# Output projection of a hybrid decoder layer: 14 of 16 column tiles by seven half-size products per pair of tiles instead of eight

## The chip, the core and the metric

One core of one Trainium2 chip runs one launch. The metric is device microseconds of that launch; here the median of three runs, with one further execution recorded by the hardware profiler. Engines by the names of the profile: PE (TensorE, with PEld for its weight loads), DVE (VectorE), ACT (ScalarE), POOL (GpSimd), SP (the queue that issues most DMAs).

## What is computed

One layer of a decoder trunk on 512 prompt tokens and 8 sample tokens (520 columns), width 2048. One input projection feeds two branches, a gated mixing of chunks (`y_a`) and a matrix-state recurrence (`y_b`); then

```python
merged = sigmoid(g_a) * (y_a @ p_a) + sigmoid(g_b) * (y_b @ p_b)
out = x + c_gate[:, None] * (merged @ w_out)
y = rmsnorm(out, final_g)
```

The change is in how `merged @ w_out` is computed, a product of 2048 x 2048 weights with 2048 x 520 values. `c_gate` is one column for the prompt and one for each of the 8 sample tokens.

## The kernel before

Values are kept transposed: 128 features by 520 tokens per tile, 16 tiles per 2048 features. Each big product is a `job`: one column tile of 128 outputs, cut into units of four k-tiles. For a unit a weight load of 128 x 8 x 128 (two units in one) comes by SP's queue into `raw`; `split_to` makes a high part by a cast on ACT (`hi`) and the rest by a subtract on DVE (`lo`, or POOL where said), both of 128x512. Per k-tile and half of the tokens (260 columns) PE does three matmuls: hi by high values, hi by low values, lo by high values. So a job with 16 k-tiles is 96 matmuls. Two PSUM banks take the two halves; an `evac` function is called for each.

The order of all instructions is written out by the program: `emit_pe` (line 401) walks the units; before the matmuls of unit i it issues the weight loads up to unit i+8, as long as one of four `raw` buffers is free, and the splits up to unit i+2 (four `hi` and four `lo` buffers). Work beside the matmuls is written as generators; `side.tick()` after each k-tile lets those go on whose time, by a table of costs in the program (`Engine.cost`, line 140), has come, and `side.drain` (line 95) runs one to its end on the spot. Every engine works its own queue in that order, and an instruction that waits holds up all behind it.

The last stages: the tail of the input projection (17 jobs of gates, beside the last pair of the recurrence and the sample task), then 16 jobs `pa` of 8 k-tiles, 16 jobs `pb` of 16, then 16 jobs `wo`. `pre_merge` (1404) drains all tasks ahead of `pa`. `evac_pb` (1443) adds the two gated branches of tile m and splits the 520 columns into `mh` and `ml`, the values for `wo`. `evac_out` (1482) does out = x + gate * product on DVE (prompt columns by one `scalar_tensor_tensor`, the 8 sample columns by two small operations), and `square` (1496) squares on ACT, scales by `final_g` and adds the square to `acc` on DVE. The first 13 `wo` jobs do both halves; the last three (`n_last`) do all first halves and then all second halves, so that the norm and the output of the first half (`final_norm(0)`, 1507, and `rows`, 1531) run beside the last three second halves. All instructions go through one helper, so that the trace gives L136 for nearly all of them; tiles tell them apart.

Of the kernel before, what the change touches and what calls it, by code (L numbers as in the profile page):

```python
# [173 lines left out]
def hybrid_step(ctx, tc, xT, cT, wc, vecs, sst, win, wlr, w2a2, stw, lnv, wsT, w00, bs, pa, pb, wo,  # L174
# [64 lines left out]
    def C(shape, name, dt=F32):  # L239
        return const.tile(list(shape), dt, name=name)  # L240
# [4 lines left out]
    hs = slots("h", 32)  # L245
    gelp = open_pool("g", "gel")
# [37 lines left out]
    def rounded(t, name):  # L284
        r = C((128, 128), name, F32R)
        V.tensor_copy(r, t)
        return r

    bones_r, vmat_r, cmat_r = rounded(bones, "bonesr"), rounded(vmat, "vmatr"), rounded(cmat, "cmatr")
    mask = C((128, 128), "mask")  # L290
# [75 lines left out]

    ptr = dict(dma=0, split=0, pe=0)
    raws = [4]

    def emit_dma(upto):  # L370
        while ptr["dma"] < min(len(units), upto):
            u = units[ptr["dma"]]
            if u["load"]:
                if not raws[0]:
                    return
                raws[0] -= 1
                src, users = u["load"]
                t = wp.tile([128, 8, 128], F32, tag="raw", bufs=4, name="raw")
# [8 lines left out]
                users[-1][0]["frees"] = True  # L387
            ptr["dma"] += 1

    def emit_split(upto):  # L390
        while ptr["split"] < min(len(units), upto):
# [4 lines left out]
            lo = wp.tile([128, u["n"], u["j"]["M"]], F32R, tag="lo", bufs=4, name="lo")  # L396
            split_to(u.pop("raw"), hi, lo, G if 22 <= n < 32 else V)
            raws[0] += u.pop("frees", 0)
            u["hl"] = (hi, lo)

    def emit_pe():
        while ptr["pe"] < len(units):
# [947 lines left out]
    tail += [(win[104 + m], gb_d[m]) for m in range(n_g, 16)]  # L1350
    for n, (w, d) in enumerate(tail):
        job(w, 16, 128, mov_h, evac_gate(d, ws), pre={0: pre_tail0, len(tail) - 2: pre_ya}.get(n))
# [7 lines left out]
    def load_ya():  # L1360

        for m in range(8):
            t = ws(name="yar")
# [3 lines left out]
        for m in range(n_early):  # L1367
            hl = ws(dt=F32R, name="yah"), ws(dt=F32R, name="yal")
# [35 lines left out]
    def pre_merge():  # L1404
        for t in list(tasks.values()):
            side.drain(t)
# [233 lines left out]
```

## Time and profile before

| | |
|---|---|
| runs | 2318.20, 2318.81, 2319.34 us (median 2318.81) |
| profiled execution | 2316.69 us, span of the core 2315.0, mean granted clock 0.996 |
| PE / PEld busy | 2268.9 / 2206.0 us (98% / 95%) |
| DVE / ACT / POOL busy | 1389.1 / 946.2 / 689.5 us (60% / 41% / 30%) |
| `pa` begins, last matmul of `wo` ends | about 1832.7, 2293.4 us |

The span is the time from the core's first to its last instruction. Matmuls overlap in the record, so their busy time says little of their rate; the interval between starts does. "Idle before, releaser" names what ended an engine's wait. One full level of the granted clock (1.00) is 2.4 GHz, 0.50 is 1.2 GHz.

### The profile page before, as it was taken

What the parts mean: (1) busy time and instruction counts of PE and PEld (TensorE: products, weight loads), DVE (VectorE), ACT (ScalarE), POOL (GpSimd) and SP (SyncE); (2) the same over time, 40 slices, a digit from 0 to 9 for tenths busy, and PEclk for the clock granted to TensorE, in tenths of its full rate; (3) what the DMA queues carried; (4) which work ended last, traced back from release to release, by engine and by line L of the source; (5) the groups of instructions that cost most, each with busy time, mean ns of one, the idle gap of its engine ahead of it and who ended that gap; (6) DMA issues with size and microseconds to landing.
All of it is one profiled execution on the core that took longest, in us unless ns stands there. A gap on an engine that the chain in (4) does not pass through costs nothing.

```text
span 2315.0 us, 52544 instructions
## 1 busy us (share of the span) xinstructions
PE 2268.9 (98%) x21339; PEld 2206.0 (95%) x21339; DVE 1389.1 (60%) x2627; ACT 946.2 (41%) x2209; POOL 689.5 (30%) x1517
## 2 busy tenths in 40 slices
PE   7999999999999999999999999999999999999996
PEld 6899999999999999999999999999999999999996
DVE  6655453336767767767767677676898433444436
ACT  4323431234445545445545455455334422223333
POOL 2420002000444423443525444155684320000001
PEclk9999999999999999999999999999999999999998
DMA  8854248432332332232323223232454643334225
GB/s 288 300 212 174 97 140 274 155 101 83 93 92 83 101 97 78 86 95 88 95 82 97 76 93 93 82 100 84 140 167 141 233 158 123 116 117 170 92 92 138
DMA packets 165537, 296.64 MB, mean 128 GB/s; under 512 B 69192, under 2 KB 86344, under 8 KB 164656
## 3 DMA queue, kind: packets, MB, share of 16 engines
q1 hardware_dynamic: 149616, 239.13, 33.2%
q0 software_dynamic: 15680, 54.16, 6.2%
q8 instruction: 168, 2.75, 0.5%
q14 instruction: 73, 0.60, 0.1%
HBM read 264.94 MB, written 28.28 MB: 127 GB/s over the span
## 4 chain that ended last, share of the span: by engine, by line
PE 79%; DVE 3%; issue 1%; POOL 0%; ACT 0%; DVEq 0%; POOLq 0%; ACTq 0%
PE acc L136 67%; PE gram L136 2%; PE y L136 2%; PE S L136 1%; PE R L136 1%; PE U L136 1%; PE lora L136 1%; PE m L136 1%; PE tk L136 1%; PE vT L136 1%; DVE st L136 1%; DVE lo L136 1%; PE t L136 0%; PE nrm L136 0%; POOL mtm L136 0%
## 5 line engine op out<-in xcount | busy, mean ns | idle before, releaser
L136 PE MATMUL acc<-hh,hi 128*128 128x260 f32 (+1 forms) x3904 | 1156.1, 296 | 4.8 <-DVE gel L136 2.3
L136 PE MATMUL acc<-hl,hi 128*128 128x260 f32 (+1 forms) x3904 | 1101.8, 282 | 0.3 <-DVE hl L136 0.3
L136 PE MATMUL acc<-hh,lo 128*128 128x260 f32 (+1 forms) x3904 | 1101.4, 282 | 0.4 <-DVE lo L136 0.4
L136 PEld LDWEIGHTS acc<-hh,hi 128*128 128x128 f32 (+1 forms) x3904 | 734.3, 188 | 28.1 <-issue 9.8
L136 PEld LDWEIGHTS acc<-hl,hi 128*128 128x128 f32 (+1 forms) x3904 | 734.8, 188 | 2.0 <-DVE hl L136 0.6
L136 PEld LDWEIGHTS acc<-hh,lo 128*128 128x128 f32 (+1 forms) x3904 | 733.2, 188 | 0.6 <-DVE lo L136 0.6
L136 DVE TENSOR_TENSOR lo<-raw,hi 128x512 fp32r<-128x512 f32 (+2 forms) x682 | 487.1, 724 | 327.5 <-ACT hi L136 323.5
L136 ACT CAST hi<-raw 128x512 fp32r<-128x512 f32 (+2 forms) x692 | 403.1, 597 | 282.2 <-PE acc L136 267.8
L136 POOL TENSOR_TENSOR mtm<-xm,mtm 128x60 f32<-128x60 f32 (+24 forms) x496 | 189.0, 381 | 137.4 <-DMA xm<-xd 103.3
L136 POOL TENSOR_TENSOR mtm<-mtm 128x60 f32<-128x60 f32 (+24 forms) x496 | 186.9, 377 | 38.8
L136 PE MATMUL acc<-mh,hi 128*128 128x260 f32 x512 | 144.6, 283 | 0.0
L136 PE MATMUL acc<-ml,hi 128*128 128x260 f32 x512 | 144.6, 282 | 0.0
L136 PE MATMUL acc<-mh,lo 128*128 128x260 f32 x512 | 144.6, 282 | 0.0
L136 POOL DMA_DIRECT2D out<-xo x4 | 3.1, 774 | 428.9 <-DVE xo L136 421.4
L136 DVE TENSOR_TENSOR gel<-gel,acc 128x260 f32<-128x260 f32 x160 | 65.3, 421 | 78.7 <-PE acc L136 78.2
L136 ACT ACTIVATE q<-acc,vec 128x260 f32<-128x260 f32 (+1 forms) x100 | 47.6, 476 | 120.9 <-PE acc L136 120.3
L136 PEld LDWEIGHTS acc<-mh,hi 128*128 128x128 f32 x512 | 96.5, 188 | 0.0
L136 PEld LDWEIGHTS acc<-ml,hi 128*128 128x128 f32 x512 | 96.4, 188 | 0.0
L136 PEld LDWEIGHTS acc<-mh,lo 128*128 128x128 f32 x512 | 96.3, 188 | 0.0
L136 ACT COPY xu<-U 64x64 f32<-64x64 f32 x256 | 52.9, 207 | 96.3 <-PE U L136 87.4
L136 PE MATMUL acc<-ybh,lo 128*128 128x260 f32 x320 | 90.3, 282 | 0.0
L136 PE MATMUL acc<-ybl,hi 128*128 128x260 f32 x320 | 90.3, 282 | 0.0
(291 smaller groups left out, 3538.1 us busy)
## 6 DMA issues: line engine op xcount, KB each, us to landing
raw<-in_win SPq DMA_DIRECT2D x240, 512.0 KB, 3.7
wcr<-in_wc POOLq DMA_DIRECT2D x57, 512.0 KB, 7.9
raw<-in_wo SPq DMA_DIRECT2D x38, 512.0 KB, 3.6
wcg<-in_wc SPq DMA_DIRECT2D x64, 256.0 KB, 5.6
raw<-in_pb SPq DMA_DIRECT2D x32, 512.0 KB, 3.7
xm<-xd SPq DMA_DIRECT2D x64, 128.0 KB, 2.7
raw<-in_pa SPq DMA_DIRECT2D x16, 512.0 KB, 3.5
x<-in_xT SPq DMA_DIRECT2D x16, 260.0 KB, 5.3
```

What stands on the lines that cost most here:

```text
L136: return f(*a, **k)
```

## The change

With the weights of a pair of column tiles a, b cut into quarters (A11, A12 the two halves of k for a, A21, A22 for b) and the merged values into quarters (b11, b12 the two halves of tokens of the first eight k-tiles, b21, b22 of the other eight), seven products of 8 k-tiles by 260 tokens replace eight:

S1 = A21+A22, S2 = S1-A11, S3 = A11-A21, S4 = A12-S2; T1 = b12-b11, T2 = b22-T1, T3 = b22-b12, T4 = b21-T2; P1 = A11 b11, P2 = A12 b21, P3 = S4 b22, P4 = A22 T4, P5 = S1 T1, P6 = S2 T2, P7 = S3 T3. With U = P1+P6: a's first half is P1+P2, a's second U+P5+P3, b's first U+P7+P4, b's second U+P7+P5.

The order is P1, P2, P6, P5, P7, P4, P3, two units of 12 matmuls each. Weight sums are done on POOL before the split, by halves; the value quarters are summed and split once, in tasks started by `evac_pb`, whose tiles now come in the order 0, 8, 1, 9, ... 25 of the split pieces are stored to DRAM, 17 of them fetched again when the output stage starts and 8 (b12) for the last two tiles, which are done as before by halves (`n_last` 2). Constants of the recurrence go to a pool of their own, which is given up with the recurrence's pool three jobs before the end of the tail; one pool `fin` then serves to the end, and brings four more `raw` buffers. x is loaded in four tiles, in the last `pb` job.

```diff
-    def C(shape, name, dt=F32):
-        return const.tile(list(shape), dt, name=name)
+    def C(shape, name, dt=F32, pool=None):
+        return (pool or const).tile(list(shape), dt, name=name)
     vec = C((128, V_N), "vec")
     SY.dma_start(out=vec, in_=vecs)
     open_pool("h", "h", "right")
     hs = slots("h", 32)
+    rwc = open_pool("rwc", "rwc")
...
+    PIECES = dict(P1=("A11", "b11"), P2=("A12", "b21"), P6=("S2", "T2"), P5=("S1", "T1"), P7=("S3", "T3"),
+                  P4=("A22", "T4"), P3=("S4", "b22"))
+    def seven(jobs, mov):
+        seq = []
+        for srcs, done in jobs:
+            j = dict(src=dict(A11=srcs[0][:, 0:8], A12=srcs[0][:, 8:16], A21=srcs[1][:, 0:8], A22=srcs[1][:, 8:16]),
+                     done=done, w={}, uses=dict(A11=6, A21=6, A22=4, A12=6, S1=4, S2=4), M=128)
+            seq += [(j, p) for p in ("P1", "P2", "P6", "P5", "P7", "P4", "P3")]
+        at = {}
+        for j, p in seq:
+            at[id(j), p] = len(units)
+            for k0 in (0, 4):
+                units.append(dict(j=j, st=p, k0=k0, n=4, first=k0 == 0, last=k0 == 4, load=None, pre=None, part=None,
+                                  mov=mov))
+        for j in {id(j): j for j, _ in seq}.values():
+            p1, p2, p6 = (at[id(j), p] for p in ("P1", "P2", "P6"))
+            for u, n in ((p1, "A11"), (p1 + 1, "A21"), (p2, "A22"), (p2 + 1, "A12")):
+                units[u]["quarter"] = n, j
+            for u, out, x, y, op, half in (
+                    (p6 - 8, "S1", "A21", "A22", OP.add, 0), (p6 - 8, "S2", "S1", "A11", OP.subtract, 0),
+                    (p6 - 7, "S1", "A21", "A22", OP.add, 1), (p6 - 7, "S2", "S1", "A11", OP.subtract, 1),
+                    (p6 - 6, "S3", "A11", "A21", OP.subtract, 0), (p6 - 5, "S3", "A11", "A21", OP.subtract, 1),
+                    (p2 - 1, "S4", "A12", "S2", OP.subtract, 0), (p2 - 1, "S4", "A12", "S2", OP.subtract, 1)):
+                units[u].setdefault("sums", []).append((j, out, x, y, op, half))
+    HOME = dict(S3="A21", S4="A12")
+    sevens = ["m0", "m1", "m2", "y", "ch"]
+    def used(j, n):
+        n = HOME.get(n, n)
+        j["uses"][n] -= 1
+        if not j["uses"][n]:
+            raw_done(j["w"][n])
+    def weight_sum(j, out, x, y, op, half):
+        if out in ("S1", "S2") and out not in j["w"]:
+            j["w"][out] = raw_tile()
+        w = j["w"]
+        k = slice(4 * half, 4 * half + 4)
+        G.tensor_tensor(w[HOME.get(out, out)][:, k, :], w[x][:, k, :], w[y][:, k, :], op)
+        used(j, x)
+        used(j, y)
...
+    raws = {"w": 4}
+    raw_home = {}
+    def raw_tile():
+        key = max(raws, key=raws.get)
+        raws[key] -= 1
+        t = (wp if key == "w" else cur[key]).tile([128, 8, 128], F32, tag="raw", bufs=4, name="raw")
+        raw_home[t.tensor.name] = key
+        return t
...
+            if (u["load"] or "quarter" in u) and sum(raws.values()) < (3 if "quarter" in u else 1):
+                return
+            if "quarter" in u:
+                n, j = u["quarter"]
+                j["w"][n] = raw_tile()
+                SY.dma_start(out=j["w"][n], in_=j["src"][n])
...
+    def seventh(u, hi, lo):
+        j, p = u["j"], u["st"]
+        if u["first"]:
+            sevens.append(sevens.pop(0))
+            j["ps"] = psum(sevens[-1], 1, "acc")
+        o = j["ps"][:, 0:HN]
+        for k in range(4):
+            mh, ml = u["mov"](PIECES[p][1], u["k0"] + k)
+            first, last = u["first"] and k == 0, u["last"] and k == 3
+            PE.matmul(o, hi[:, k, :], mh, start=first, stop=False)
+            PE.matmul(o, hi[:, k, :], ml, start=False, stop=False)
+            PE.matmul(o, lo[:, k, :], mh, start=False, stop=last)
+            side.tick()
+        if u["last"]:
+            j["done"](p, o)
...
+            for a in u.get("sums", ()):
+                weight_sum(*a)
...
+    def pre_last_home():
+        for t in list(tasks.values()):
+            side.drain(t)
+        cur.pop("wkv").release()
+        cur.pop("rwc").release()
+        open_pool("fin", "fin")
+        raws["fin"] = 4
+        V.tensor_scalar(mod[:, 32:48, :], mod[:, 32:48, :], 0.5, None, OP.mult)
...
+            pre={0: pre_tail0, len(tail) - 3: pre_last_home, len(tail) - 2: pre_ya}.get(n))
...
+    piece, resting = {}, {}
+    SPILLED = [("T3", k) for k in range(7)] + [("T4", k) for k in range(7)] + [("b22", k) for k in range(4, 7)]
+    SPILLED += [("b12", k) for k in range(8)]
+    def keep(n, k, src, eng):
+        t = (fs if (n, k) in SPILLED or n in ("b22", "T3", "T4") else ms)((128, 2, HN), F32R, name=n)
+        split_to(src, t[:, 0], t[:, 1], eng)
+        if (n, k) in SPILLED:
+            resting[n, k] = dram.tile([128, 2, HN], F32, name=f"{n}d{k}")
+            side.unawaited(lambda: SY.dma_start(out=resting[n, k], in_=t.bitcast(F32)))
+        else:
+            piece[n, k] = t
+    def back(n, k):
+        piece[n, k] = t = (ms if n == "b12" else fs)((128, 2, HN), F32R, name=n)
+        SY.dma_start(out=t.bitcast(F32), in_=resting[n, k])
+    def quarters(k, x, y):
+        b11, b12, b21, b22 = x[:, 0:HN], x[:, HN:N], y[:, 0:HN], y[:, HN:N]
+        t = fs((128, 2, HN), name="t12")
+        t1, t2 = t[:, 0], t[:, 1]
+        u = fs((128, 2, HN), name="t34")
+        t3, t4 = u[:, 0], u[:, 1]
+        keep("b11", k, b11, V)
+        G.tensor_tensor(t1, b12, b11, OP.subtract)
+        keep("b21", k, b21, V)
+        yield
+        V.tensor_tensor(t2, b22, t1, OP.subtract)
+        yield
+        keep("T2", k, t2, V)
+        keep("T1", k, t1, V)
+        G.tensor_tensor(t3, b22, b12, OP.subtract)
+        G.tensor_tensor(t4, b21, t2, OP.subtract)
+        yield
+        keep("T3", k, t3, G)
+        yield
+        keep("T4", k, t4, G)
+        yield
+        keep("b22", k, b22, G)
+        yield
+        keep("b12", k, b12, G)
+    def mov_piece(n, k):
+        side.draining = True
+        while (n, k) not in piece:
+            side.clock["PE"] += 333.0
+            side.tick()
+        side.draining = False
+        t = piece[n, k]
+        return t[:, 0], t[:, 1]
+    def mov_half(k, hf):
+        return mov_piece(("b11", "b12", "b21", "b22")[k // 8 * 2 + hf], k % 8)
...
+            V.tensor_tensor(g[:, sl], g[:, sl], m1[m][:, sl], OP.add)
             if hf == 1:
-                gate_t.pop(m)
-                V.tensor_tensor(g, g, m1[m], OP.add)
                 m1[m] = None
-                hi, lo = ms(dt=F32R, name="mh"), ms(dt=F32R, name="ml")
-                A.activation(hi, g, AF.Copy, scale=0.5)
-                V.scalar_tensor_tensor(lo, g, 0.5, hi.bitcast(F32), OP.mult, OP.subtract)
-                mg[m] = (hi, lo)
+                if m >= 8:
+                    side.add(quarters(m - 8, gate_t.pop(m - 8), gate_t.pop(m)))
...
+    for n in range(16):
+        m = n // 2 + n % 2 * 8
+        job(pb[m], 16, 128, lambda k: ybT[k], evac_pb(m), pre=pre_pb(n, m))
...
+    units[-3]["pre"] = load_x(0, 1)
+    units[-2]["pre"] = load_x(2, 3)
...
+        G.memset(fin["acc"], 0.0)
+        A.activation(zero8, zero8, AF.Sqrt)
+        tasks["back"] = side.add(reload())
+    def reload():
+        for i, (n, k) in enumerate(SPILLED[:-8]):
+            while (n, k) not in resting:
+                yield "t"
+            back(n, k)
+            if i % 2:
+                yield "t"
...
+    def part_out(m, hf, o, last=True):
+        sl = slice(hf * HN, hf * HN + HN)
+        n = min(HN, T - hf * HN)
+        a = slice(hf * HN, hf * HN + n)
+        x = fin["x"][m // 4][:, m % 4]
+        V.scalar_tensor_tensor(x[:, a], o[:, 0:n], mod[:, 32 + m, 0:1], x[:, a], OP.mult, OP.add)
+        if n < HN:
+            t = cur["fin"].tile([128, NS], F32, tag="gs", bufs=4, name="gs")
+            V.tensor_tensor(t, o[:, n:HN], mod[:, 32 + m, 1:9], OP.mult)
+            G.tensor_tensor(x[:, T:N], x[:, T:N], t, OP.add)
+        if last:
+            close(m, hf)
...
+    def close(m, hf):
+        sl = slice(hf * HN, hf * HN + HN)
+        tasks["sq", m, hf] = side.add(square(m, fin["x"][m // 4][:, m % 4, sl], fin["acc"][:, sl], hf))
...
-            V.tensor_tensor(acc, acc, q, OP.add)
+            (G if m < 14 and m % 2 else V).tensor_tensor(acc, acc, q, OP.add)
+    def done_out(a, b):
+        st = {}
+        def scaled(m, t, u, sample):
+            s8 = None
+            if sample:
+                s8 = cur["fin"].tile([128, NS], F32, tag="gs", bufs=4, name="gs")
+                G.tensor_tensor(s8, u[:, T - HN:HN], mod[:, 32 + m, 1:9], OP.mult)
+            A.activation(t, u, AF.Identity, scale=mod[:, 32 + m, 0:1])
+            return t, s8
+        def add(m, hf, t, s8):
+            x = fin["x"][m // 4][:, m % 4]
+            n = min(HN, T - hf * HN)
+            G.tensor_tensor(x[:, hf * HN:hf * HN + n], x[:, hf * HN:hf * HN + n], t[:, 0:n], OP.add)
+            if hf:
+                G.tensor_tensor(x[:, T:N], x[:, T:N], s8, OP.add)
+            close(m, hf)
+        def later(f):
+            yield
+            f()
+        def e(p, o):
+            if p == "P1":
+                st["u"] = fs((128, HN), name="u")
+                A.copy(st["u"], o)
+                part_out(a, 0, o, False)
+            elif p == "P2":
+                part_out(a, 0, o)
+            elif p == "P6":
+                V.tensor_tensor(st["u"], st["u"], o, OP.add)
+                st["a"] = fs((128, HN), name="gu")
+                side.add(later(lambda: st.update(a=scaled(a, st["a"], st["u"], True))))
+            elif p == "P5":
+                part_out(a, 1, o, False)
+                part_out(b, 1, o, False)
+            elif p == "P7":
+                V.tensor_tensor(st["u"], st["u"], o, OP.add)
+                def f():
+                    st["b"] = scaled(b, st["u"], st["u"], True)
+                    add(b, 1, *st["b"])
+                tasks["add", b] = side.add(later(f))
+            elif p == "P4":
+                part_out(b, 0, o, False)
+                side.drain(tasks["add", b])
+                add(b, 0, *st["b"])
+            else:
+                part_out(a, 1, o, False)
+                add(a, 1, *st["a"])
+        return e
...
-    n_last = 3
-    for m in range(16 - n_last):
-        job(wo[m], 16, 128, lambda k: mg[k], evac_out(m), pre=pre_out(m))
+    def pre_plain():
+        for k in range(8):
+            back("b12", k)
+    n_last = 2
+    n0 = len(units)
+    seven([((wo[m], wo[m + 1]), done_out(m, m + 1)) for m in range(0, 16 - n_last, 2)], mov_piece)
+    units[n0]["pre"] = pre_out
     for hf in range(2):
         for m in range(16 - n_last, 16):
-            job(wo[m], 16, 128, lambda k: mg[k], evac_out(m), hfs=(hf,),
-                pre=pre_last if hf and m == 16 - n_last else pre_out(m))
+            job(wo[m], 16, 128, None, evac_out(m), hfs=(hf,),
+                pre={(0, 14): pre_plain, (1, 14): pre_last}.get((hf, m)))
+            for u in units[-4:]:
+                u["j"]["half"] = mov_half
```

## Rows read from the trace of the kernel before

**Rows 1.** Page, part 1: busy time, share of the span, instructions of each engine.
```profile
PE 2268.9 (98%) x21339; PEld 2206.0 (95%) x21339; DVE 1389.1 (60%) x2627; ACT 946.2 (41%) x2209; POOL 689.5 (30%) x1517
```

**Rows 2.** Chain that ended last, 1700 to 2315: start, us, what.
```profile
1832.70 443.06 PE acc L136 x3692
...
2276.79 16.58 PE acc L136 x138
```

**Rows 3.** Windows: length, busy and instructions of PE, PEld, DVE, ACT, POOL; clock, DMA share, GB/s.
```profile
60.00:70.00 10.00, 8.00 (x61) 7.29 (x61) 9.93 (x28) 5.20 (x14) 5.23 (x9) 1.00 0.89 323
...
1700.00:1800.00 100.00, 96.03 (x877) 93.82 (x876) 87.25 (x121) 37.26 (x82) 56.91 (x61) 1.00 0.48 154
...
2000.00:2100.00 100.00, 100.00 (x837) 100.00 (x836) 41.16 (x71) 25.09 (x44) 0.00 (x0) 1.00 0.35 114
```

**Rows 4.** Groups by shape, DVE, 2130 to 2290: busy us, mean ns | idle before, releaser.
```profile
L136 DVE TENSOR_TENSOR lo<-raw,hi 128x512 fp32r<-128x512 f32 x66 | 45.1, 688 | 36.3 <-ACT hi L136 36.3
...
L136 DVE SCALAR_TENSOR_TENSOR xo<-acc,mod,xo 128x260 f32<-128x260 f32 x15 | 7.3, 489 | 41.3 <-PE acc L136 41.3
```

**Rows 5.** Groups by shape, ACT, 2130 to 2290.
```profile
L136 ACT CAST hi<-raw 128x512 fp32r<-128x512 f32 x66 | 40.0, 614 | 35.3 <-PE acc L136 34.4 <-DVE xo L136 0.8
L136 ACT ACTIVATE xo<-xo,vec 128x260 f32<-128x260 f32 x29 | 14.9, 513 | 0.9
L136 ACT ACTIVATE osq<-xo 128x260 f32<-128x260 f32 x29 | 12.2, 422 | 62.7 <-DVE xo L136 62.7
```

**Rows 6.** Timeline, POOL: start, us, instruction [idle before, releaser].
```profile
1844.71 1.76 POOL L136 TENSOR_TENSOR ybw<-ybr,ybw 128x520 fp32r<-128x520 f32 x1
...
1846.56 1.31 POOL L136 TENSOR_TENSOR ybw<-ybr,ybw 128x520 fp32r<-128x520 f32 x1
1847.82 0.18 POOL L136 COPY ybr<-ybs 128x8 f32<-128x8 f32 x1
...
2296.08 2.39 POOL L136 TENSOR_TENSOR xo<-xo,rs 128x1040 f32<-128x1040 f32 x1
```

**Rows 7.** Timeline, DVE and POOL, around 1635.
```profile
1634.13 2.85 DVE L136 TENSOR_TENSOR lo<-raw,hi 128x512 fp32r<-128x512 f32 x1
...
1634.37 2.05 POOL L136 TENSOR_TENSOR st<-st 128x512 f32<-128x512 f32 x2
```

**Rows 8.** Groups by shape, DVE: 1835 to 1862 (two), then 1900 to 2100 (two).
```profile
L136 DVE TENSOR_TENSOR lo<-raw,hi 128x512 fp32r<-128x512 f32 x11 | 11.0, 1031 | 0.0
L136 DVE SCALAR_TENSOR_TENSOR m<-gld,acc 128x260 f32<-128x260 f32 x10 | 4.2, 423 | 11.9 <-PE acc L136 11.9
...
L136 DVE TENSOR_TENSOR lo<-raw,hi 128x512 fp32r<-128x512 f32 x70 | 45.3, 687 | 31.6 <-ACT hi L136 31.6
...
L136 DVE SCALAR_TENSOR_TENSOR m<-gld,acc 128x260 f32<-128x260 f32 x9 | 3.8, 425 | 15.8 <-PE acc L136 15.8
```

**Rows 9.** Timeline, SP, at the start of the output projection.
```profile
2107.68 1.98 SPq L136 DMA_DIRECT2D xo<-in_xT  x4
```

**Rows 10.** Windows, DMA at the start of the output projection (last two columns).
```profile
2112.00:2114.00 2.00, 2.00 (x19) 2.00 (x18) 1.90 (x3) 1.23 (x4) 0.00 (x0) 1.00 1.00 424
```

**Rows 11.** Timeline, ACT, DVE and PE, around the end of the sample task.
```profile
1796.39 0.39 ACT L136 ACTIVATE gt<-acc 128x260 f32<-128x260 f32 x1 [1.01 <-PE acc L136]
...
1796.42 0.53 DVE L136 TENSOR_SCALAR say<-say,sbmv,srs 128x64 f32<-128x64 f32 x2
...
1798.71 0.27 PE L136 MATMUL ysT<-ident,say 128*128 128x128 f32 x1
```

**Rows 12.** Timeline, DVE and POOL, behind the last matmul.
```profile
2294.07 0.69 DVE L136 TENSOR_TENSOR xo<-xo,rs 128x520 f32<-128x520 f32 x1
...
2298.76 0.80 POOL L136 DMA_DIRECT2D out<-xo  x1 [0.30 <-POOL xo L136]
```

**Rows 13.** Windows, the end (DMA share is the last but one column).
```profile
2302.00:2305.00 3.00, 0.00 (x0) 0.00 (x0) 2.97 (x4) 0.00 (x0) 1.79 (x1) 0.50 1.15 230
...
2308.00:2311.00 3.00, 0.00 (x0) 0.00 (x0) 0.00 (x0) 0.00 (x0) 0.00 (x0) 0.50 1.24 198
```

More of the change, by code (lines that the diff above doesn't have):

```diff
@@ L289, in hybrid_step @@
     bones_r, vmat_r, cmat_r = rounded(bones, "bonesr"), rounded(vmat, "vmatr"), rounded(cmat, "cmatr")
-    mask = C((128, 128), "mask")
+    mask = C((128, 128), "mask", pool=rwc)
     V.memset(mask, 1.0)
@@ L420, in emit_pe @@
             hi, lo = u.pop("hl")
+            if "st" in u:
+                seventh(u, hi, lo)
+                continue
             if u["first"]:
@@ L1350, in hybrid_step, with four @@
     tail += [(win[104 + m], gb_d[m]) for m in range(n_g, 16)]
+    NF_S = 31
+    def pre_last_home():
[6 more added lines that the diff above has]
+        V.tensor_scalar(mod[:, 32:48, :], mod[:, 32:48, :], 0.5, None, OP.mult)
+    fs = slots("fin", NF_S)
+    def four(name, dt=F32):
+        return cur["fin"].tile([128, 4, N], dt, tag="W", bufs=4, name=name)
     for n, (w, d) in enumerate(tail):
-        job(w, 16, 128, mov_h, evac_gate(d, ws), pre={0: pre_tail0, len(tail) - 2: pre_ya}.get(n))
+        job(w, 16, 128, mov_h, evac_gate(d, lambda **k: (fs if "fin" in cur else ws)(**k)),
+            pre={0: pre_tail0, len(tail) - 3: pre_last_home, len(tail) - 2: pre_ya}.get(n))
     yaT, ybT, mg = [None] * 8, [None] * 16, [None] * 16
@@ L1389, in load_yb @@
         ld = [load(0)]
+        w = None
         for p in range(HP):
@@ L1394, in load_yb @@
             yield 1500.0
-            if p < 6:
-                w = wide("ybw", F32R, 2 * N)
-                hi, lo = w[:, 0:N], w[:, N:2 * N]
+            if p < 8:
+                w = w if p % 2 else four("ybw", F32R)
+                hi, lo = w[:, 2 * (p % 2)], w[:, 2 * (p % 2) + 1]
             else:
-                hi, lo = ws(dt=F32R, name="ybh"), ws(dt=F32R, name="ybl")
+                hi, lo = fs(dt=F32R, name="ybh"), fs(dt=F32R, name="ybl")
             A.copy(hi, t)
@@ L1404, in pre_merge @@
     def pre_merge():
-        for t in list(tasks.values()):
-            side.drain(t)
+        side.drain(tasks["ya"])
         cur["h"].release()
@@ new lines, in hybrid_step, with load_x, pre_out @@
+    fin = {"x": [None] * 4}
+    def load_x(*gs_):
+        def f():
+            for g in gs_:
+                fin["x"][g] = four("xo")
+                SY.dma_start(out=fin["x"][g], in_=xT[:, 4 * g:4 * g + 4, :])
+        return f
+    units[-3]["pre"] = load_x(0, 1)
+    units[-2]["pre"] = load_x(2, 3)
+    def pre_out():
+        ybT.clear()
+        fin["acc"] = fs(name="acc")
+        fin["rs"] = fs(name="rs")
+        G.memset(fin["acc"], 0.0)
+        A.activation(zero8, zero8, AF.Sqrt)
+        tasks["back"] = side.add(reload())
@@ L1504, in square @@
         if m < 15:
-            V.tensor_tensor(acc, acc, q, OP.add)
+            (G if m < 14 and m % 2 else V).tensor_tensor(acc, acc, q, OP.add)
[42 more added lines that the diff above has]
+                add(b, 0, *st["b"])
+            else:
+                part_out(a, 1, o, False)
+                add(a, 1, *st["a"])
+        return e
     def final_norm(hf):
         rs = fin["rs"][:, hf * HN:hf * HN + HN]
-        side.drain(tasks["sq", 14, hf])
+        for m in range(15):
+            side.drain(tasks["sq", m, hf])
         yield from grab()
@@ L1555, in hybrid_step @@
     side.drain(side.add(final_norm(1)))
-    cur["out"].release()
+    cur["fin"].release()
     cur["mrg"].release()
```

92 lines of the change are left out of this document (35 added, 57 removed).

## The prediction, made before the changed kernel was run

> **What bounds the kernel now.** I read the busy lines of the page first: TensorE is busy for 98% of the span [rows 1]. The chain of waits shows where that is the bound: from 1832.70 us to the last matmul it is one unbroken run of TensorE, broken only by the reduction of the first half's norm, and behind it stand 21.6 us of normalising and storing that TensorE has no part in [rows 2]. So a matmul taken out of that run is worth its issue interval, as long as whatever feeds TensorE keeps up. The windows give the interval: 837 matmuls in 100.00 us, 0.1195 us each, at granted clock 1.00 [rows 3]. In the same window VectorE is busy for 41 us of 100 and GpSimd for none. The output projection therefore runs with GpSimd empty; the change fills it.
>
> **What goes.** 14 column tiles cost 14 x 96 = 1344 matmuls, 160.6 us, or 22.9 us per pair. Seven products of 24 matmuls are 168 per pair, 20.1 us, and 140.5 us for seven pairs. 20.1 us are saved if nothing else waits. The same number of weight loads goes with them. The count follows from the code, so that the products are really fewer isn't in question.
>
> **What comes, per pair.** Weight splits rise from 8 to 14, each a ScalarE cast of 0.61 us and a VectorE subtract of 0.69 us [rows 4, 5]: 8.6 and 9.7 us of 20.1, and a unit of weights now lasts 12 matmuls, 1.43 us, instead of 2.87. VectorE's evacuations are six at 0.49, two at about 0.43 and three of 8 columns: about 4.3 us. ScalarE has four squares (0.42) and four scalings (0.51) as before, and two scalings and a copy more [rows 5]: 13.7 us in all. Both fit into 20.1.
>
> GpSimd gets eight half sums of 128x512. Two neighbouring starts of its 128x520 subtract lie 1.26 us apart; 128x1040 takes 2.39 [rows 6], so by the slope 128x260 is about 0.70, an estimate from these two. Eight sums 10.1, three adds and two norm sums of 128x260 3.5, seven pieces of 8 columns at 0.18 [rows 6] 1.3: 14.9 us.
>
> **GpSimd and VectorE get in each other's way.** A VectorE subtract that starts at 1634.13 lasts 2.85 us instead of 0.69: it ends just after the two GpSimd products that ran from 1634.37 to 1636.42 [rows 7]. The other way, the GpSimd subtract goes from 1.31 to 1.76 when a VectorE subtract falls in: 0.45 [rows 6]. Operations with one operand in PSUM are spared: 423 ns beside a busy GpSimd, 425 beside an idle one, while the subtracts go from 687 to 1031 [rows 4, 8]. So each of 14 splits and two norm sums adds up to 0.45 us to GpSimd's 14.9: 22.1 us per pair, already over TensorE's 20.1. The Trainium skill (SBUF — State Buffer, Who interferes with whom) calls this an exclusive lock, held for the whole instruction by a VectorE operation with two SBUF inputs. By that sentence each collision would cost GpSimd 0.69 and not 0.45; with the five collisions counted below that makes 1.2 us more per pair and a time of about 2339.
>
> **Where it reaches TensorE.** The order of the queues decides. From the end of the fourth product (P5), in us, one unit being 1.43: VectorE needs 1.3 for P5's two evacuations, GpSimd 0.2 more, so S1 and S2 of the next pair (first halves) run from 1.5 to 4.0. Only behind them stands what P7's evacuation needs: small product 0.18, ScalarE's scaling 0.51, add 0.70, small add 0.18, done at 5.6. The square of that result is queued on ScalarE ahead of the cast for P3's second unit, as ScalarE now sits waiting on squares (62.7 us of idle before 29 of them) [rows 5]. Square, scaling, cast and subtract are 0.42 + 0.51 + 0.61 + 0.69 = 2.23: ready at 7.8, wanted at 7.2. Then S1 and S2 (second halves), the add behind P4, ready at 8.8, and 2.23 later, at 11.0, the second unit of the next P1, wanted at 10.0. Then S3's two halves, a norm sum and the adds behind P3: 13.1, and at 15.3 the second unit of the next P2, wanted at 12.9. So without one collision TensorE stands still for 2.4 us per pair: 22.5 us, which nearly gives back the whole gain. With all seven splits of that stretch colliding it is 3.2 us later, and the last subtract waits half a sum (0.6): 6.2, or 26.3 per pair. Below, nothing would wait: 20.1. I take five collisions (TensorE's stalls thin out the splits): 5.3, or 25.4 per pair, nearer to the upper end because [rows 7, 8] show collisions wherever both engines work. During the stalls GpSimd catches up, so they don't add up from pair to pair.
>
> The last pair has no next sums. GpSimd is then free when P7 ends, and the same chain (0.42 + 0.18 + 0.51 + 0.70 + 0.18 + 2.23 = 4.2 behind P7, 4.3 allowed) just fits: 20.3.
>
> Stage: 6 x 25.4 + 20.3 = 172.7 against 160.6: **12.1 us more**.
>
> **The other edits.** Merging (the stage of the second branch): eight pieces per pair of tiles instead of two splits; TensorE has 22.9 us per pair there, VectorE about 59 us of 100 free [rows 3], GpSimd seven operations of 0.70; nothing waits. 25 stores of pieces enter SP's queue, each waiting for GpSimd's subtract; behind them stand gate loads and weight loads, which are asked for eight units (23 us) ahead: 0, at most 2 if a gate comes late. Input x is now asked for 8.6 and 5.7 us before the products of the branch end, once its space is read out; behind it stand 17 pieces to be fetched back (4.5 MB). SP takes 1.98 us for four such issues [rows 9], and the DMA moved 424 GB/s here [rows 10]: 4.3 + 4.5 MB in 20.7 us, so the last lands at some 13 to 15 us, wanted from 11.5 (P7) to 19.4 (P3's end): 0, up to 8 us if the rate halves. The pool that is given up three tiles earlier drains the sample task there: its transpose on TensorE comes at 1798.71 behind a VectorE operation that ends at 1796.95 [rows 11]; asked for at 1796.4, it waits 0.6 (0 to 1.5). Memory that moves between pools costs no time of its own.
>
> **The end.** Two tiles instead of three run by halves at the end, so the first half's norm has 11.5 instead of 17.2 us of matmuls over it. Today its last VectorE multiply starts at 2294.07, after the last matmul, and its last store at 2298.76 [rows 12]. Now four multiplies (2.4 us) and three stores fall behind the last matmul; VectorE reaches the second half's reciprocal about 0.8 us later, and half a megabyte more goes through a DMA that is full at the end (shares 1.15 and 1.24) [rows 13]: 1.0 (0 to 3).
>
> **Sum**, on the profiled execution's own time (2316.69; its span is 2315.0): 12.1 + 0.6 + 1.0 = 13.7, 2330.4. The median shown is 2318.81, 2.1 above that execution, so 2332.
>
> **Rivals.**
> - **TensorE stays the bound (faster).** The casts come in time, since GpSimd runs ahead of where I put it or the squares stand later on ScalarE. The point: the add behind P7 must be done 4.9 us after P5's end, and the one behind P3 10.7 after. For it: in 1700:1800 VectorE was busy for 87% and GpSimd for 57% and TensorE lost only 4 us of 100 [rows 3]. Against: there GpSimd's work wasn't queued ahead of weight casts. 20.1 saved, 5.6 lost at that rate, 1.6 for the edits: 2306 (2300 with no loss).
> - **Queue order without collisions:** 6 x 22.5 + 20.3 = 155.3, 5.3 saved, 1.6 lost: 2315. Against it rows 7 and 8; for it that sums running ahead of need may fall between the splits.
> - **The pieces come back late** on top of the forecast: SP waits for space or stores, the rate halves, 8 us more: 2340. For it the burst of 8.8 MB; against it 424 GB/s.
> - That the stalls lower TensorE's clock is no case of mine: a window with TensorE busy for 8.00 of 10 us kept 1.00 [rows 3], the same share as 20.1 of 25.4.
>
> **How the numbers follow.** Forecast 0.55 (own range 2322 to 2342), TensorE-bound 0.20, no collisions 0.15, late pieces 0.10. 0.2%, 4.6 us, is about what a measurement here can tell from no change. Faster: 0.20 and 0.05 of the no-collision case, 0.25. Same: 0.08 of that case and 0.04 of the forecast's lower edge, 0.12. Slower: 0.63. 2304 to 2345 leaves out some 0.08 on either side.
>
> **What would show it.** Right: in the stage of the seven products TensorE's idle time is put down to VectorE's `lo` or ScalarE's `hi`, ScalarE's idle time to GpSimd's `x`, twice or three times per pair; VectorE's 128x512 subtracts average near 1 us; GpSimd is busy for over 80%. Wrong: TensorE without gaps there (the first rival), subtracts still at 0.69 (the second), or gaps before T3, T4 or b22 in the first pair alone (the third). If the seventh pair is as slow as the others, the sums aren't the cause.

## The result, and the profile after

2354.82 us, the median of four runs, against 2318.51 beside them: ratio 1.0153 [1.0135, 1.0171]. Slower, as forecast, but by 36 us where 13.7 were predicted, and outside the range. A second measurement of the same kernel, on the chip of the second series of experiments, gave 1.0138 [1.0123, 1.0153].

The busy lines against [rows 1]: 168 matmuls fewer, GpSimd 178 us busier, and TensorE no busier than before in a longer span.

```profile
PE 2270.2 (96%) x21171; PEld 2197.2 (93%) x21171; DVE 1460.3 (62%) x2710; ACT 987.4 (42%) x2316; POOL 867.4 (37%) x1716
```

The windows of the output projection, cut where P6 of each pair starts (the third product in order), so that a row is one period of seven products. Of the last three rows the first holds the last pair's P6 to P3 and the first half of the two plain tiles, the second their second half, the third the end. Columns as in [rows 3]; the line by itself is the stage before, by the same cut (up to the norm's matmul behind the last product).

```profile
2121.42:2153.10 31.68, 24.28 (x171) 22.95 (x169) 17.75 (x29) 14.14 (x30) 22.62 (x26) 0.89 0.51 195
2153.10:2180.32 27.22, 21.94 (x170) 20.51 (x169) 16.19 (x28) 12.43 (x25) 17.26 (x21) 1.00 0.25 78
2180.32:2208.06 27.74, 23.10 (x170) 21.76 (x169) 16.77 (x28) 12.41 (x25) 17.22 (x21) 0.94 0.23 76
2208.06:2235.13 27.07, 22.01 (x171) 20.56 (x169) 16.05 (x28) 12.44 (x25) 17.27 (x21) 1.00 0.25 79
...
2288.94:2318.87 29.93, 28.27 (x223) 26.87 (x222) 17.72 (x36) 15.38 (x30) 6.80 (x13) 1.00 0.52 195
2318.87:2330.77 11.90, 11.90 (x97) 11.55 (x96) 8.24 (x15) 5.13 (x10) 1.37 (x2) 1.00 0.01 1
2330.77:2353.00 22.23, 1.31 (x6) 0.49 (x4) 12.68 (x13) 1.41 (x3) 8.38 (x7) 0.60 0.87 192
```
```profile
2107.96:2293.20 185.24, 185.24 (x1542) 184.88 (x1541) 84.38 (x176) 73.26 (x140) 1.54 (x2) 1.00 0.36 124
```

A period should last 20.1 us and lasts 31.7 once, then 26.9 to 27.7. The stage runs from 2115.66 to 2330.77, 215.1 us; before it lasted 185.2. So 29.9 of the 38.0 us between the two profiled executions arise here. The end costs 0.4 more (22.2 for 21.8), the earlier drain 0.9, the two stages behind the drain 0.3. The other 6.5 stand in the profile before the first changed instruction (the last product of the group norm runs at 1781.58 instead of 1775.03); the run of the changed kernel again, below, shows that most of them go with the execution.

Who waits, by shape, in the five periods from 2153.10 to 2288.94 (VectorE, ScalarE, GpSimd, TensorE; columns as in [rows 4]):

```profile
L136 DVE TENSOR_TENSOR lo<-raw,hi 128x512 fp32r<-128x512 f32 x71 | 65.0, 927 | 51.9 <-ACT hi L136 51.9
...
L136 ACT ACTIVATE osq<-xo 128x260 f32<-128x260 f32 x20 | 8.4, 421 | 46.3 <-POOL xo L136 34.1 <-DVE xo L136 12.2
...
L136 POOL TENSOR_TENSOR raw<-raw 128x512 f32<-128x512 f32 x41 | 54.0, 1323 | 7.8 <-DVE lo L136 4.3 <-DMA raw<-in_wo 2.0 <-ACT hi L136 0.7
L136 POOL TENSOR_TENSOR acc<-acc,osq 128x260 f32<-128x260 f32 x10 | 9.7, 967 | 0.0
...
L136 PE MATMUL acc<-b,hi 128*128 128x260 f32 x241 | 47.6, 294 | 11.7 <-ACT hi L136 11.7
...
L136 PE MATMUL acc<-b,lo 128*128 128x260 f32 x121 | 36.3, 300 | 12.1 <-DVE lo L136 12.0
```

Nearly all of TensorE's idle time (23.8 of 24.9 us) stands at the products with plain `b` pieces (P3, P1, P2), behind `hi` and `lo`; ScalarE waits in front of its squares (`osq`) for GpSimd's `xo`. That is the chain of the prediction. One turn of it, in the fourth period (timeline, the three feeding engines and the matmul that is released):

```profile
2224.52 0.47 DVE L136 SCALAR_TENSOR_TENSOR xo<-acc,mod,xo 128x260 f32<-128x260 f32 x1
...
2225.07 1.12 POOL L136 TENSOR_TENSOR xo<-xo,u 128x260 f32<-128x260 f32 x1 [1.02 <-DVE xo L136]
2226.16 2.51 POOL L136 TENSOR_TENSOR raw<-raw 128x512 f32<-128x512 f32 x2
2226.23 0.42 ACT L136 ACTIVATE osq<-xo 128x260 f32<-128x260 f32 x1 [2.73 <-POOL xo L136]
2226.68 0.51 ACT L136 ACTIVATE xo<-xo,vec 128x260 f32<-128x260 f32 x1
2227.10 1.12 ACT L136 CAST hi<-raw 128x512 fp32r<-128x512 f32 x2
2227.74 1.48 DVE L136 TENSOR_TENSOR lo<-raw,hi 128x512 fp32r<-128x512 f32 x1 [2.14 <-ACT hi L136]
...
2229.14 0.47 DVE L136 SCALAR_TENSOR_TENSOR xo<-acc,mod,xo 128x252 f32<-128x252 f32 x1
2229.27 0.39 PE L136 MATMUL acc<-b,lo 128*128 128x260 f32 x1 [1.01 <-DVE lo L136]
```

The chain closes on itself, as a ring: evacuation, GpSimd's add, square, cast, `lo`, and behind `lo` in VectorE's queue the evacuation of the *next* product, which had been ready since TensorE went on to the product after it (2227.76). One turn takes 4.62 us (2224.52 to 2229.14) where a product takes 2.87. `lo` lasts 1.48 because GpSimd's two sums hold on until 2228.67.

### The profile page after: what moved, and what is told of

Same layout as the page of the kernel before. It is cut to its first block, busy times and chain, and to the rows that moved or that the text cites. A ratio compares the mean times of both kernels' runs of the same rounds, so it can differ in the third digit from the quotient of the medians.

```text
span 2353.0 us, 52825 instructions
## 1 busy us (share of the span) xinstructions
PE 2270.2 (96%) x21171; PEld 2197.2 (93%) x21171; DVE 1460.3 (62%) x2710; ACT 987.4 (42%) x2316; POOL 867.4 (37%) x1716
## 4 chain that ended last, share of the span: by engine, by line
PE 67%; POOL 5%; DVE 5%; issue 3%; ACT 2%; DMA 2%; DVEq 0%; SPq 0%; POOLq 0%; ACTq 0%
PE acc L136 55%; PE gram L136 2%; DVE lo L136 2%; POOL mtm L136 2%; PE y L136 1%; POOL raw L136 1%; PE S L136 1%; PE R L136 1%; PE U L136 1%; PE lora L136 1%; ACT hi L136 1%; POOL xo L136 1%; PE m L136 1%; DVE xo L136 1%; POOL ss L136 1%
## 5 line engine op out<-in xcount | busy, mean ns | idle before, releaser
L136 DVE TENSOR_TENSOR lo<-raw,hi 128x512 fp32r<-128x512 f32 (+2 forms) x720 | 543.6, 763 | 362.0 <-ACT hi L136 358.2
L136 ACT CAST hi<-raw 128x512 fp32r<-128x512 f32 (+3 forms) x730 | 425.1, 599 | 311.7 <-PE acc L136 286.6
L136 PE MATMUL acc<-b,hi 128*128 128x260 f32 x464 | 91.2, 295 | 17.3 <-ACT hi L136 17.3
L136 PEld LDWEIGHTS acc<-b,hi 128*128 128x128 f32 x464 | 74.5, 196 | 21.3 <-ACT hi L136 21.2
L136 PE MATMUL acc<-ybw,hi 128*128 128x260 f32 x512 | 92.7, 282 | 0.0
L136 DVE SCALAR_TENSOR_TENSOR sh<-acc,omu,q 128x260 f32<-128x260 f32 (+1 forms) x100 | 47.9, 486 | 63.5 <-ACT shifts L136 32.1
L136 ACT COPY rs<-R 128x128 f32<-128x128 f32 x128 | 34.0, 265 | 118.8 <-PE R L136 117.8
L136 PE MATMUL acc<-b,lo 128*128 128x260 f32 x232 | 69.3, 299 | 14.0 <-DVE lo L136 14.0
L136 PE MATMUL acc<-T,hi 128*128 128x260 f32 x448 | 81.1, 282 | 0.0
L136 POOL TENSOR_TENSOR raw<-raw 128x512 f32<-128x512 f32 x56 | 74.5, 1336 | 17.8 <-DVE lo L136 11.0
```

Source lines behind the costliest of these rows:

```text
L136: return f(*a, **k)
```

## The experiments

Each ratio is against runs of the kernel before in the same series; e11_write and e12_aside rest on two runs each. Beside the ratios stand the periods, read from the trace in the same way (us; "later" is the usual period after the first; "last" runs from the end of the last P4 to the end of the plain tiles' first half). In e6_v_path and e7_v_path_g the second period is longer than the usual one, 26.4 and 27.6:

| kernel | ratio [95%] | first | later | last |
|---|---|---|---|---|
| after | 1.0153 [1.0135, 1.0171] | 31.7 | 27.0 | 18.0 |
| e1_pools | 1.0004 [0.9995, 1.0012] | – | – | – |
| e2_late_sq | 1.0058 [1.0045, 1.0072] | 28.9 | 24.2 | 15.0 |
| e3_no_sums | 1.0020 [1.0009, 1.0030] | 23.1 | 23.1 | 18.0 |
| e4_no_fetch | 1.0132 [1.0115, 1.0149] | 29.0 | 26.9 | 18.0 |
| e5_late_no_sums | 0.9919 [0.9904, 0.9933] | 20.3 | 20.1 | 15.0 |
| e6_v_path | 1.0034 [1.0020, 1.0049] | 23.3 | 23.8 | 15.0 |
| e7_v_path_g | 1.0036 [1.0021, 1.0050] | 22.5 | 24.2 | 15.0 |
| e8_again | 1.0138 [1.0123, 1.0153] | 32.4 | 26.9 | 18.0 |
| e9_even | 1.0076 [1.0060, 1.0093] | 28.8 | 24.4 | 15.0 |
| e10_sums_v | 0.9984 [0.9974, 0.9994] | 25.7 | 21.5 | 15.0 |
| e11_write | 1.0099 [1.0078, 1.0120] | 31.4 | 24.4 | 18.0 |
| e12_aside | 1.0143 [1.0116, 1.0170] | 32.7 | 26.8 | 18.0 |

**The pools alone** (the kernel before, its constants moved):

```diff
-    def C(shape, name, dt=F32):
+    def C(shape, name, dt=F32, pool=None):
...
```


> The kernel before, with nothing but the constants of the recurrence moved to a pool of their own, as the change has it, so that later tiles lie at other addresses; same instructions in the same order. The trace of the changed kernel is 6.5 us late by 1775 us, where its instructions still stand in the order of before. If the addresses are the cause: 2325, 6 to 7 us over before. If it is something else (another placement in DRAM, or a difference between executions): 2318, no change.

Nothing: the placement isn't the cause.

**Squares later** (after, each square of a paired tile 12 k-tiles later in the queues):

```diff
     def square(m, x, acc, hf):
+        for _ in range(12 if m < 14 else 0):
+            yield "t"
         yield
```


> The changed kernel, with the squares of the output projection put into ScalarE's queue twelve k-tiles (three units) later, so that weight casts are not queued behind squares that wait for GpSimd's adds. Theory of the prediction (GpSimd's work reaches TensorE through ScalarE's queue): the pair goes from 27.2 us to 22.5 to 24, total 2330 to 2338. Rival (the subtracts of VectorE, held up by GpSimd at the shared port, set the pace): the pair stays at 26 to 27, total above 2348.

2.8 us per period come back, and all 3.0 of the last part: the ring is opened by taking the square out from ahead of the cast. The 24.2 left is a little over the range expected. GpSimd is then the busiest engine beside TensorE (18.62 of 24.28); that its load is the bound isn't shown, and the runs below that take work from it speak against it:

```profile
2154.00:2178.28 24.28, 21.67 (x166) 20.11 (x165) 17.50 (x27) 11.63 (x25) 18.62 (x20) 1.00 0.24 81
```

**No weight sums** (after, products take plain quarters, so its output is another):

```diff
...
-        G.tensor_tensor(w[HOME.get(out, out)][:, k, :], w[x][:, k, :], w[y][:, k, :], op)
...
```


> The changed kernel without the eight weight sums per pair: the products use the loaded quarters in place of S1 to S4, so the output is not the reference's; splits, products and evacuations are all there. If the sums on GpSimd are what delays the adds and subtracts: 20.1 to 21.5 us per pair, total 2312 to 2322. If the chain through the adds alone is long enough to stall the casts: 22 to 24 per pair, total 2325 to 2337. If neither: 27 per pair, 2354.

23.1, with `lo` back at 0.69. The ring still costs 3.0 us per period with no sum in it, and the first period no longer differs. One turn there:

```profile
2178.84 0.48 DVE L136 SCALAR_TENSOR_TENSOR xo<-acc,mod,xo 128x260 f32<-128x260 f32 x1
...
2179.41 1.12 POOL L136 TENSOR_TENSOR xo<-xo,u 128x260 f32<-128x260 f32 x1 [2.71 <-DVE xo L136]
...
2180.56 0.42 ACT L136 ACTIVATE osq<-xo 128x260 f32<-128x260 f32 x1 [1.84 <-POOL xo L136]
...
2181.43 1.12 ACT L136 CAST hi<-raw 128x512 fp32r<-128x512 f32 x2
2182.07 0.69 DVE L136 TENSOR_TENSOR lo<-raw,hi 128x512 fp32r<-128x512 f32 x1 [2.14 <-ACT hi L136]
...
2182.68 0.47 DVE L136 SCALAR_TENSOR_TENSOR xo<-acc,mod,xo 128x252 f32<-128x252 f32 x1
```

3.84 us for 2.87, with GpSimd idle before the add: no engine is full, the order of the queues is the whole loss.

**No storing and fetching** (after, the 25 pieces alias others, so its output is another):

```diff
-            side.unawaited(lambda: SY.dma_start(out=resting[n, k], in_=t.bitcast(F32)))
...
```


> The changed kernel without storing and fetching back 25 split pieces: products that would use them take other resident pieces (T1, T2, b21, b11), so the output is not the reference's. If the fetch is what makes the first pair 4.6 us longer than the others and leaves 3.7 us of gaps in the last two tiles: 8 us less, 2347. If the weight sums would hold those products up anyway: under 2 us less, 2353 to 2355.

Neither branch: 2.7 us (3.4 against the changed kernel run again), in the first period alone, and the last part stays at 18.0. The median falls where the first branch put it, but the ratio can't be told from the 1.0138 of the changed kernel run again.

**Both, squares later and no sums**:

> The changed kernel without the eight weight sums of a pair (the products multiply whole quarters of the weight in their place, so the output is another) and with the squares of an output tile put into the queues 12 k-tiles later: the two edits tried singly before (27.1 us per pair became 24.3 by the later squares and 23.1 without the sums). Theory (ScalarE's and GpSimd's queue order, and VectorE slowed by GpSimd's sums, make up the whole stall): nothing is left, 20.1 to 20.8 us per pair, 7 x 2.5 us under the 2321.5 us without sums, 2302 to 2308 us. Rival (a third cause, such as the weight quarters that land late or a PSUM bank that is freed late): 22 us per pair or more, 2314 us or more.

```profile
2137.60:2238.13 100.53, 100.53 (x842) 100.53 (x841) 69.27 (x135) 62.22 (x126) 38.53 (x60) 1.00 0.30 106
```

TensorE is never idle and the period is the 20.1 of the count (the time came 3 us under the range expected). No third cause is left in the later periods.

**The output path on VectorE** (both with the squares later), once with the sums of squares there too, once with them on GpSimd:

```diff
-                side.add(later(lambda: st.update(a=scaled(a, st["a"], st["u"], True))))
+                part_out(a, 1, st["u"], False)
...
```


> The changed kernel with the squares 12 k-tiles later and the whole way from a product to the output tile on VectorE: the sum u of products is scaled and added by scalar_tensor_tensor straight from u, ScalarE's scaled copies and GpSimd's additions (samples, halves, sums of squares) are gone; GpSimd keeps the weight sums alone, 8 x 1.32 = 10.6 us of a pair. Theory (GpSimd's queue is the bound since the squares went later): 20.5 to 22 us per pair, 2303 to 2314 us. Rival (VectorE, with 14 splits of 0.69 to 1.04 us, 14 evacuations and sums of 0.43, four squares' sums and ten sample steps of 0.2, 18 to 22 us of a pair, becomes the bound): 22.5 to 24.5 us, 2317 to 2331 us, with TensorE idle for lo.

> As the kernel with the output path on VectorE, but all four sums of squares of a pair on GpSimd (4 x 0.97 us), which then has 14.5 us of a pair, VectorE 16.5 to 20. Theory (balance of the two queues decides): 20.3 to 21.5 us per pair, 2302 to 2311 us, under the kernel before. Rival (VectorE's splits still slowed to 0.93 us and more by GpSimd reading memory): 22 us or more, 2315 us or more.

Both miss: the rivals were right. In the first VectorE is the bound (91.19 us busy of 95.23), and at least 17 us of that are GpSimd's doing: 57 `lo` at 0.99 instead of 0.69. An evacuation that reads `u` from SBUF takes 0.69 to 1.00, one from PSUM 0.47.

```profile
L136 DVE TENSOR_TENSOR lo<-raw,hi 128x512 fp32r<-128x512 f32 x57 | 55.0, 992 | 0.0
...
L136 DVE SCALAR_TENSOR_TENSOR xo<-acc,mod,xo 128x252 f32<-128x252 f32 x12 | 5.7, 474 | 0.4
...
L136 DVE SCALAR_TENSOR_TENSOR xo<-u,mod,xo 128x252 f32<-128x252 f32 x8 | 5.6, 694 | 0.3
L136 DVE SCALAR_TENSOR_TENSOR xo<-u,mod,xo 128x260 f32<-128x260 f32 x4 | 4.0, 1001 | 0.1
```

**The changed kernel again:**

> The changed kernel unaltered, beside the others. If what the profiled execution lost before the output projection (6.5 us by the end of the gates) belongs to that execution: the last gate product ends at 1774 to 1779 us and the stage alone makes the difference, 27.1 us per pair again. If it belongs to the change: 1781 us again. In either case 27 us per pair and 2347 to 2356 us.

The last product of the group norm runs at 1776.17 this time, 1.1 us from before's, and the stage lasts 214.7 us again. So at least 5.4 of the 6.5 belong to the execution. What makes them was not found; over all kernels, whose instructions are the same up to there, that product lay between 1775.0 and 1783.3. The two profiles without the change (before and e1_pools) have it earliest, at 1775.0 and 1775.9, and all twelve with it at 1776.2 or later, so that a small part of the lag may be the change's after all.

**Memsets in place of the sums, and sums that nobody waits for**:

```diff
...
+        for n in (N, N, 128):
+            G.memset(d[:, 0:n], 0.0)
```
```diff
...
+        G.tensor_tensor(d, w[HOME.get(x, x)][:, k, :], w[HOME.get(y, y)][:, k, :], OP.add)
```


> The changed kernel with each of the eight weight sums of a pair replaced by three memsets of a spare tile (1168 columns, estimated at 1.1 to 1.4 us from the 0.97 us of a 128x1024 memset in the profile of before): GpSimd is as long occupied at the same place of its queue, but reads nothing and nobody waits for what it writes (the products use whole quarters, so the output is another). If what the sums cost is GpSimd's queue: about 26 to 27 us per pair. If it is the collision of GpSimd's reads with VectorE's: lo stays at 0.69 us and 23 to 24 us per pair, as without sums. Both in parts: between.

> The changed kernel with the eight weight sums still made by GpSimd from the same quarters, but into a spare tile that nobody waits for (the products use whole quarters, so the output is another). Queue and collisions are as in the changed kernel, only the wait of the splits for a sum is gone. If that wait (a sum late behind a quarter that lands late, or behind GpSimd's queue) is what costs: 23 to 24.5 us per pair. If collisions and queue cost it without the wait: 26 to 27 us. Against the kernel with memsets: what is over its period is the price of GpSimd's reading, and lo should be 0.93 us here.

Three memsets take GpSimd 1.27 us, nearly what a sum takes, and leave `lo` at 0.73; the sums into a spare tile take 1.42 and bring it to 0.89:

```profile
L136 POOL MEMSET dum<- 128x520 f32 x48 | 25.6, 532 | 2.1
...
L136 POOL MEMSET dum<- 128x128 f32 x24 | 4.9, 205 | 1.4
...
L136 DVE TENSOR_TENSOR lo<-raw,hi 128x512 fp32r<-128x512 f32 x42 | 30.0, 726 | 30.3 <-ACT hi L136 30.0
```
```profile
L136 POOL TENSOR_TENSOR dum<-raw 128x512 f32<-128x512 f32 x32 | 45.3, 1417 | 1.3
...
L136 DVE TENSOR_TENSOR lo<-raw,hi 128x512 fp32r<-128x512 f32 x56 | 49.3, 892 | 41.5 <-ACT hi L136 41.5
```

So of a later period's 6.9 us, 3.0 are the ring without sums (23.1 - 20.1), 1.3 the time of the sums in GpSimd's queue (24.4 - 23.1), 2.4 their reading (26.8 - 24.4; it includes what little GpSimd waits for a quarter, 1.3 us of 107), and 0.1 to 0.2 that a split waits for its sum. The parts depend on the order in which they are taken out: with the sums still there, the later squares gave 2.8 and not 3.0. The first period of the memsets, 31.4, doesn't fit that ledger (the spare tile also takes one of the places into which pieces are fetched); it is left open.

**Shared out evenly, and the sums on VectorE** (both with the squares later):

```diff
-            G.tensor_tensor(x[:, T:N], x[:, T:N], t, OP.add)
+            V.tensor_tensor(x[:, T:N], x[:, T:N], t, OP.add)
...
-            (G if m < 14 and m % 2 else V).tensor_tensor(acc, acc, q, OP.add)
+            V.tensor_tensor(acc, acc, q, OP.add)
```


> The changed kernel with the squares 12 k-tiles later, and with all sums of squares and the sample additions of the evacuations on VectorE instead of GpSimd (about 1.5 us per pair more for VectorE, 2 x 0.97 + 5 x 0.37 = 3.8 us less for GpSimd). Theory (with both queues near 18 to 20 us of a pair GpSimd's was the bound): 21.5 to 23 us per pair, 2310 to 2320 us. Rival (what one engine gives up the other loses to collisions): 24 us or more, 2326 us or more.

```diff
-        G.tensor_tensor(w[HOME.get(out, out)][:, k, :], w[x][:, k, :], w[y][:, k, :], op)
+        V.tensor_tensor(w[HOME.get(out, out)][:, k, :], w[x][:, k, :], w[y][:, k, :], op)
...
```


> The changed kernel with the squares 12 k-tiles later, the eight weight sums of a pair on VectorE (8 x 0.69 us at the price of a split without a collision) and all sums of squares on GpSimd. VectorE then has 14 x 0.69 + 8 x 0.69 + 8 x 0.45 + 0.5 = 19.3 us of a pair, GpSimd 7 us. Theory (collisions are what makes the two engines slow, so the same work on one engine is quicker than on two): 20.3 to 22 us per pair, 2302 to 2313 us, under the kernel before. Rival (VectorE, waiting in order for quarters that land late, is the bound): 24 us or more, 2325 us or more.

The even split gains nothing over the late squares (24.4; `lo` at 1.17 us): the rival was right. Work taken from GpSimd's queue and given to VectorE's is worth nothing here while the sums stay on GpSimd. With the sums on VectorE, though that was nearly as busy as GpSimd (17.50 and 18.62 us with late squares), and all sums of squares on GpSimd, the period falls to 21.5, and the kernel is faster than before, 2311.64 us against 2315.73, by 0.16%, the interval just clear of 1:

```profile
2163.49:2249.73 86.24, 84.61 (x674) 81.42 (x673) 78.17 (x133) 50.73 (x101) 47.50 (x57) 1.00 0.31 99
```
```profile
L136 DVE TENSOR_TENSOR lo<-raw,hi 128x512 fp32r<-128x512 f32 x57 | 43.4, 783 | 2.0 <-ACT hi L136 2.0
L136 DVE TENSOR_TENSOR raw<-raw 128x512 f32<-128x512 f32 x32 | 26.0, 822 | 0.3
```

VectorE is busy for 78.17 of 86.24 us and does more in less time: `lo` takes 0.78 us where it took 1.06 with late squares alone, now that GpSimd's sums are out of its way. That GpSimd's queue became shorter by the same edit is a rival which no run separates from this, though the even split shortened it too and gained nothing.

## Why the prediction was right in direction and wrong in size

- **What goes** held: 20.1 us per pair when nothing waits (squares later and no sums). That GpSimd stands empty in the output projection was read in a window of the stage before it (2000:2100), but it is so: 1.54 us busy of 185.24.
- **Where it reaches TensorE**: the point was right to the instruction (square ahead of the cast, behind GpSimd's add), and so were the signs of it: TensorE's idle time at `lo` and `hi`, ScalarE's at GpSimd's `xo`, `lo` at 0.93 us. One sign was not: GpSimd was to be busy for over 80% and was for 64%:

```profile
2153.10:2288.94 135.84, 110.99 (x843) 103.87 (x841) 80.74 (x136) 62.17 (x125) 86.39 (x101) 0.99 0.24 78
```

  So GpSimd's load, which the prediction put at up to 22.1 us per pair and which measured 17.3, isn't what sets the pace; the ring does. The failing sentences are two. "So without one collision TensorE stands still for 2.4 us per pair": 4.3 with memsets in the queue, and 3.0 with no sums at all, where the working gives none. It took each product's evacuation as ready when the product ends; in fact it stands behind the late `lo` in VectorE's queue, so lateness is handed from P4 to P3 to the next P1. "During the stalls GpSimd catches up, so they don't add up" is true from pair to pair (26.9 to 27.7, no growth) and false within one.
- **"I take five collisions: 5.3"**: the collisions as such were near, 2.4 for the 2.9 taken. With the ring it makes 6.9 instead of 5.3.
- **The first pair** was priced like the others and took 4.7 more. 2.7 go with the fetching (without it 29.0). The other 2.0 stay open; without fetching GpSimd is busy for 22.96 us of that period, against 17.3 in a later one, since it still works on the last merged tiles' pieces there, which the prediction let end with the branch:

```profile
2123.12:2152.12 29.00, 23.25 (x170) 21.80 (x169) 18.62 (x29) 14.14 (x30) 22.96 (x26) 0.94 0.16 55
```

  Of the fetching, the third rival looked at the right place, SP's queue, but at the wrong load: its 17 pieces kept the DMA full to 2134.55 (the first window under the dismissed case, share 1.04), and the next pair's weight quarters, asked for behind them at 2126.78, landed only then; GpSimd waited:

```profile
2126.78 2.29 SPq L136 DMA_DIRECT2D raw<-in_wo  x4
...
2135.16 1.28 POOL L136 TENSOR_TENSOR raw<-raw 128x512 f32<-128x512 f32 x1 [2.99 <-DMA raw<-in_wo]
```

- **The last pair**, "just fits", didn't: 18.0 where 15.0 are possible, in every kernel with the squares ahead and in none with them later. That the seventh pair stalls without sums was to show that the sums aren't the cause; for these 3.0 us, the ring's own, it does.
- **The dismissed case**, that stalls lower the clock, occurred. TensorE was busy for 1.71 of 5.45 us (it waited 4.74 at a stretch), and in the next 6 us the granted clock was 0.57, most of it at the lower level of 1.2 GHz:

```profile
2127.00:2134.55 7.55, 7.55 (x66) 7.55 (x65) 5.59 (x13) 3.73 (x8) 4.38 (x6) 1.00 1.04 408
2134.55:2140.00 5.45, 1.71 (x15) 1.50 (x13) 0.00 (x0) 1.00 (x3) 4.14 (x6) 1.00 0.42 167
2140.00:2146.00 6.00, 4.18 (x17) 3.88 (x18) 2.88 (x4) 3.23 (x7) 4.89 (x5) 0.57 0.01 3
```

```profile
2141.00 0.80 PE L136 MATMUL acc<-b,hi 128*128 128x260 f32 x2 [4.74 <-ACT hi L136]
```

  Its 17 matmuls took 4.18 us of TensorE instead of 17 x 0.1195 = 2.03 [rows 3]: at most 2.1 us. Little of it was lost: from one matmul released by `lo` to the next such one it was 4.71 us (2142.62 to 2147.33), against 4.62 in the fourth period. The run of the changed kernel again shows it better. There the clock fell in every later period, and four of them still lasted 26.9 us each:

```profile
2160.37:2268.13 107.76, 92.64 (x674) 87.83 (x673) 63.72 (x108) 49.69 (x101) 69.38 (x80) 0.94 0.23 79
```

  TensorE was busy for 86% of the time instead of 82% and waited that much less. The window that the dismissal rested on [rows 3] has no wait over 0.68 us in it; the case came all the same, and in the later periods it cost next to nothing. Why the clock fell in these periods of one execution and hardly in those of the other, with the same waits, isn't shown.
- **Sum of the stage**, predicted 12.1, measured 29.9. The difference of 17.8, within 0.1: five later periods 135.8 - 5 x 25.4 = 8.8, first 31.7 - 25.4 = 6.3, last 3.0 - 0.2 = 2.8. The drain (0.6) measured 0.9. The end (1.0) measured 0.4 between the two profiles, but it lasts 21.8 and 20.3 us in the two profiles with three tiles by halves and 20.6 to 22.2 in those with two, so its price isn't settled. These parts make some 31.5 of the 36 us. In the profiled execution the rest lies before the stage; whether it does in the other runs isn't shown.
- **Rivals**: TensorE-bound needed another queue order, and not that alone: it came true with late squares and no sums together. Queue order without collisions, 22.5, is the run with memsets, 24.4.

## What to carry to other kernels

Before giving work to an idle engine, look for a ring: where a late instruction stands in an in-order queue ahead of the evacuation that feeds the next such instruction, one small delay comes back with every product, with no engine full, and moving the instruction that waits longest (here the squares) behind the casts opened it. Here eight large sums with two operands in SBUF were better put on VectorE than left to GpSimd beside it, as long as VectorE's own time held them (78.17 of 86.24 us); one run shows this. And a burst of fetches is paid for by the loads that stand behind it in the queue.

## What the runs showed of the hardware

A small instruction of GpSimd that meets a running subtract of VectorE lasts until just behind its end: one of 8 columns takes 0.20 us alone and 0.58 here, ending 0.06 us after `lo` (without sums):

```profile
2174.44 0.68 DVE L136 TENSOR_TENSOR lo<-raw,hi 128x512 fp32r<-128x512 f32 x1
...
2174.60 0.58 POOL L136 TENSOR_TENSOR gs<-u,mod 128x8 f32<-128x8 f32 x1 [1.77 <-DVE u L136]
...
2176.49 0.20 POOL L136 TENSOR_TENSOR xo<-xo,gs 128x8 f32<-128x8 f32 x1
```

The other way, `lo` of 1.48 us above ends 0.55 after GpSimd's sums. So the prediction's 0.18 for a small piece was a price without company; it measured 0.37 to 0.39 on the mean. The memsets, which read nothing, left `lo` at 0.73. The Trainium skill (SBUF — State Buffer, Who interferes with whom) speaks of an exclusive lock, and says that a VectorE instruction with two SBUF inputs contends with a GpSimd instruction that reads SBUF, not with one that only writes it. The prediction weighed the lock against 0.45 us from one row; these rows agree with the page.
